# Opening tiles of a two-layer decoder trunk: the norm vector's two rows on another queue, and another order of the first tiles' work

## The chip, the cores and the metric

One core of one Trainium2 chip runs the whole program in one launch. The metric is the device time of that program in microseconds (us): the median of the runs shown, beside one profiled execution whose trace is read here. TensorE (PE in the profile) multiplies, VectorE (DVE) and ScalarE (ACT) do elementwise work, GpSimd (POOL) a little, and SyncE (SP) issues most loads. Each engine works its own list of instructions in order and waits for others by semaphores.

## The reference

A trunk of two layers on 512 tokens of width 1024, in float32. Each layer is a mixer, a cross-attention into 256 memory tokens and a SwiGLU feed-forward block, each with an RMS norm before and after it. The first layer's mixer is what the change is in:

```python
def fox_shortconv_mixer(h, w_in, b_f, conv_w, w_out):      # h = rmsnorm(x, g_mix_pre[0])
    proj = h @ w_in
    ...
    q, k, v, f_logit, b_gate, c_gate, u = jnp.split(proj, [i1, i2, i3, i4, i5, i6], axis=-1)
    ...
    log_f = jax.nn.log_sigmoid((f_logit + b_f).astype(jnp.float32))
    y_a = forgetting_attention(heads(q), heads(k), heads(v), log_f).reshape(bsz, seq, FOX_WIDTH)
    y_b = b_gate * causal_depthwise_conv(c_gate * u, conv_w)
    return jnp.concatenate([y_a, y_b], axis=-1) @ w_out
```

## The kernel before

Every float32 product is made of three products of rounded parts: high part times high part, high times low and low times high. In this stretch the names are `hTh` and `hTl` for the high and low part of the normed tokens (transposed), and `wh` and `wl` for those of the weights. ACT makes a high part by a cast, DVE makes the low part by subtracting it from the source.

The program begins with the value projection (`v`) of the first mixer, token tile by token tile (four tiles of 128 tokens, `x[0]` to `x[3]`). For a tile the squares are summed (half on ACT in `sumsq`, half on DVE), `rstd` raises the mean to the power -1/2 on POOL, `scaled` multiplies by that and by the norm's gain (DVE, tile `h`), and `put_T` transposes the eight 128x128 blocks on PE into two banks of four and splits each bank into `hTh` and `hTl`. The gain is needed on all 128 partitions: its two halves are loaded as two single rows into the tile `grow`, and two PE products with the 0/1 tile `pick` copy them to all partitions.

The weights of this projection come in four loads of 512 KB (`raw[0]`, `raw[2]`, `raw[4]`, `raw[6]`, tile `st`), each for two blocks of 128 rows. `whi_v(k0)` casts one of them on ACT (`wh`), `wlo_v(k0)` makes its low part on DVE (`wl`), and `mm_v(k0, t, which)` multiplies tile `t` with it: `h` is high by high, `x` is the low tokens by the high weights, `w` the high tokens by the low weights, two matmuls of 512 columns each, 24 for a tile. `warm_up(n)` is `n` transposes of a constant whose result nobody reads.

In this opening PE, ACT and DVE work in the order in which the Python code is written. From the gate logits on (`setup_chan` and what follows) only PE still does; the orders of ACT and DVE are there a scheduler's, which places instructions by its own estimates, so that an edit in the opening moves some of them too.

Behind the opening, the gate logits are one small product (tile `wf`), whose result ACT copies to `e` and DVE adds to `z`; the log-sigmoid and the running sum over the tokens follow on DVE (`log1p`, then a scan), the sum goes to DRAM (`cum`) by a POOL DMA, and for each pair of heads two POOL DMAs bring rows of it back to all partitions (`cb`). The first attention scores on PE fill banks that DVE empties with the help of `cb`. At the same time PE works through the `q`, `k` and convolution projections, whose results ACT and DVE split (`qk`).

Of the kernel before, what the change touches and what calls it, by code (L numbers as in the profile page):

```python
# [12 lines left out]
ALU = mybir.AluOpType  # L13
# [4 lines left out]
D = 1024  # L18
KT = D // P
# [14 lines left out]
WARM2 = 4  # L34
# [8 lines left out]
def trunk_kernel(ctx: ExitStack, tc: tile.TileContext, a: dict, out: bass.AP):  # L43
# [4 lines left out]
    nc = tc.nc  # L48
# [24 lines left out]
    def sbuf(name, n=512):  # L73
        return sp.tile([P, 516], F32, tag="s", name=name)[:, :n]

    def f(ap):
        return ap.bitcast(F32)
# [7 lines left out]
        out=mask, in_=mask, compare_op=ALU.is_ge, fill=1e30, base=0,  # L85
# [3 lines left out]
    grow = sbuf("grow")  # L89
# [9 lines left out]
    x = [xpool.tile([P, D], F32, name=f"x{t}", tag=f"x{t}") for t in range(NT)]  # L99

    def load_x(t):
        nc.sync.dma_start(out=x[t], in_=a["x"][0, t * P:(t + 1) * P, :])
# [16 lines left out]
    def load_raw(w, k0, nk, c0, c):  # L119
        st = wst.tile([P, nk, c], F32, tag="st", name="st")  # L120
        pace(nc.sync.dma_start(
            out=st, in_=w.rearrange("(k p) n -> p k n", p=P)[:, k0:k0 + nk, c0:c0 + c]
        ))
        return st
# [96 lines left out]
    def sumsq(src, acc):  # L221
        nc.scalar.activation(out=junk, in_=src, func=AF.Square, accum_out=acc)

    def rstd(st):

        nc.vector.tensor_scalar(
            out=st[:, 2:3], in0=st[:, 0:1], scalar1=1.0 / D, scalar2=EPS,
            op0=ALU.mult, op1=ALU.add,
        )
        nc.vector.scalar_tensor_tensor(  # L230
            out=st[:, 3:4], in0=st[:, 1:2], scalar=1.0 / D, in1=st[:, 2:3],
            op0=ALU.mult, op1=ALU.add,
        )
        pool[0] = nc.gpsimd.tensor_tensor(out=st[:, 4:5], in0=st[:, 3:4], in1=nhalf, op=ALU.pow).ins
        return st[:, 4:5]

    def stats(name):
        return tiny.tile([P, 8], F32, tag="st", name=name)

    def row_stats(xt, both=False):  # L240

        st = stats("pre")
        for hf in range(2):
            src = xt[:, hf * 512:(hf + 1) * 512]
            if both and hf:
                nc.vector.tensor_tensor_reduce(
                    out=sbuf("sq"), in0=src, in1=src, scale=1.0, scalar=0.0, op0=ALU.mult, op1=ALU.add,
                    accum_out=st[:, hf:hf + 1],
                )
            else:  # L250
                sumsq(src, st[:, hf:hf + 1])
        return rstd(st)

    def scaled(xt, g, r):

        hs = []
        for hf in range(2):
            h = sbuf("h")
            sl = slice(hf * 512, (hf + 1) * 512)
            nc.vector.scalar_tensor_tensor(  # L260
                out=h, in0=xt[:, sl], scalar=r, in1=g[hf], op0=ALU.mult, op1=ALU.mult
            )
            hs.append(h)
        return hs
# [10 lines left out]
    def new_hT():  # L275
        hi = [group("hTh") for _ in range(2)]
        lo = [group("hTl") for _ in range(2)]
        ft = Feat([hi[k // 4][:, k % 4, :] for k in range(KT)], [lo[k // 4][:, k % 4, :] for k in range(KT)])
        ft.ghi, ft.glo, ft.raw = hi, lo, None
        return ft  # L280
# [8 lines left out]
    def dst_T(hT, hf, t):  # L289
        if hT.hi:  # L290
            sl = slice(t * P, (t + 1) * P)
            return hT.ghi[hf][:, :, sl], hT.glo[hf][:, :, sl]
        q, c = hT.quads[hf][t // 2], t % 2 * P
        return q[:, :, c:c + P], q[:, :, 256 + c:256 + c + P]
# [5 lines left out]
        q = hT.quads[k // 4][half][:, k % 4, :]  # L300
        return q[:, 0:256], q[:, 256:512]

    def put_T(hT, t, hs, bank=bankB):
        for hf in range(2):
            ps = bank()
            for j in range(4):
                nc.tensor.transpose(
                    out=ps[:, j * P:(j + 1) * P], in_=hs[hf][:, j * P:(j + 1) * P], identity=ident
                )
            v = ps.rearrange("p (k c) -> p k c", k=4)  # L310
            sl = slice(t * P, (t + 1) * P)
            if hT.raw:
                nc.scalar.copy(out=hT.raw[hf][:, :, sl], in_=v)
            hi, lo = dst_T(hT, hf, t)
            last = (
                nc.scalar.copy(out=hi, in_=v).ins,  # L316
                nc.vector.tensor_tensor(out=lo, in0=v, in1=f(hi), op=ALU.subtract).ins,  # L317
            )
        return last
# [904 lines left out]
    def fox(proj):  # L1224
        w = a["ab_w_in"][0]
# [3 lines left out]
        hT = new_hT()  # L1229
# [6 lines left out]
        def warm_up(n):  # L1236
            for _ in range(n):
                nc.tensor.transpose(out=warm[:, 0:P], in_=ident, identity=ident)
# [4 lines left out]
        def mm_v(k0, t, which="hxw"):  # L1243

            ts = slice(t * P, (t + 1) * P)
            wh, wl = wv[k0]
            for c in which:
                for kk in range(2):
                    k = k0 + kk
                    passes[t] += 1  # L1250
                    nc.tensor.matmul(
                        out=banks[t], lhsT=(hT.lo if c == "x" else hT.hi)[k][:, ts],
                        rhs=(wl if c == "w" else wh)[:, kk, :], start=passes[t] == 1, stop=passes[t] == 3 * KT
                    )
            if passes[t] == 3 * KT:
                dst = vhl[t].rearrange("p (m s d) -> p m s d", s=4, d=64)
                src = banks[t].rearrange("p (m s d) -> p m s d", s=2, d=64)
                split_out(src, dst[:, :, 0::3, :], dst[:, :, 1:3, :])

        with tc.manual_schedule(engines={PE, mybir.EngineType.Activation, mybir.EngineType.DVE}):  # L1260
            load_x(0)
            for hf in range(2):
                nc.sync.dma_start(out=grow[32 * hf:32 * hf + 1], in_=a["g_mix_pre"][0:1, hf * 512:hf * 512 + 512])
            raw = {}
            for k0 in range(0, KT, 2):
                raw[k0] = load_raw(w, k0, 2, 2 * FOXW, 512)
                if k0 == 2:
                    load_x(1)
            load_x(2)
            load_x(3)  # L1270

            def whi_v(k0):
                hi = whi.tile([P, 2, 512], F32R, tag="wh", name="wh")
                lo = wlo.tile([P, 2, 512], F32R, tag="wl", name="wl")
                wv[k0] = hi, lo
                nc.scalar.copy(out=hi, in_=raw[k0])

            def wlo_v(k0):
                nc.vector.tensor_tensor(out=wv[k0][1], in0=raw[k0], in1=f(wv[k0][0]), op=ALU.subtract)

            nc.scalar.activation(out=junk[:, 0:1], in_=nhalf, func=AF.Square)
            g = bankB(), bankB()
            for hf in range(2):
                nc.tensor.matmul(out=g[hf], lhsT=pick[:, hf * P:hf * P + P], rhs=grow, start=True, stop=True)
            r = row_stats(x[0], True)
            nc.vector.tensor_copy(out=identb, in_=ident)
            hs = scaled(x[0], g, r)
            whi_v(0)
            wlo_v(0)
            put_T(hT, 0, hs)  # L1290
            warm_up(WARM2)
            mm_v(0, 0, "hwx")
            whi_v(2)
            r = row_stats(x[1], True)
            wlo_v(2)
            mm_v(2, 0, "hx")
            warm_up(WARM2)
            whi_v(4)
            mm_v(4, 0, "hx")
            hs = scaled(x[1], g, r)  # L1300
            wlo_v(4)
            mm_v(2, 0, "w")
            whi_v(6)
            put_T(hT, 1, hs)
            r = row_stats(x[2])
            mm_v(6, 0, "hx")
            wlo_v(6)
            hs = scaled(x[2], g, r)
            mm_v(0, 1, "hw")
            mm_v(2, 1, "hw")  # L1310
            mm_v(0, 1, "x")
            mm_v(2, 1, "x")
            mm_v(4, 0, "w")
            mm_v(4, 1)
            put_T(hT, 2, hs)
            r = row_stats(x[3])
            hs = scaled(x[3], g, r)
            mm_v(6, 0, "w")
            mm_v(6, 1)
            for k0 in range(0, KT - 2, 2):  # L1320
                mm_v(k0, 2)
            put_T(hT, 3, hs)
            mm_v(KT - 2, 2)
            for k0 in range(0, KT, 2):
                mm_v(k0, 3)
# [8 lines left out]
        for k in range(KT):  # L1334
# [5 lines left out]
            out=z, in0=ps[0:H], scalar=bf, in1=e, op0=ALU.add, op1=ALU.add  # L1340
# [5 lines left out]
            out=z, in0=z, scalar=0.0, in1=e, op0=ALU.min, op1=ALU.subtract  # L1346
# [3 lines left out]
            out=e, data0=t1, data1=z, initial=0.0, op0=ALU.mult, op1=ALU.add  # L1350
# [251 lines left out]
    hT = prev = None  # L1602
    for layer in range(2):
# [24 lines left out]
        hT = new_hT() if layer == 0 else None  # L1628
# [27 lines left out]
```

## Time and profile before

| | |
|---|---|
| median of 3 runs | 1387.04 us (1386.40 to 1387.37) |
| the profiled execution, its time | 1386.62 us |
| its span, first to last instruction | 1384.8 us |
| PE busy in the span | 1374.3 us (99%) |
| DVE, ACT, POOL busy | 80%, 52%, 8% |
| granted TensorE clock, mean | 0.998 of full speed |

The span is what the trace covers; 1.8 us of the execution's own time lie around it. Shares of busy time are means over the whole span. For a change in one place the timeline of that place is what counts, and whether the time won or lost there is still there at the end.

### The profile page before, as it was taken

To read this page: it belongs to the slowest core of one execution; us is meant where nothing else is said; L and a number is where in the kernel's file an instruction comes from. 1 tells how busy PE (TensorE), PEld (TensorE's weight loads), DVE (VectorE), ACT (ScalarE), POOL (GpSimd) and SP (SyncE) were. 2 spreads that over 40 slices of the span, in tenths; PEclk is the share of its full clock that TensorE was granted. 3 is DMA by queue.
4 is the path that set the end of the run, shared out by engine and by line. 5 is a ranking of instruction groups with operands and counts; after the bars stand their busy time and mean duration, and the time that the engine had idled before them with its cause. 6 is when DMAs were issued, how large, how long until landed. Compare 5 with 4: busy or idle time off the path is not lost.

```text
span 1384.8 us, 21780 instructions
## 1 busy us (share of the span) xinstructions
PE 1374.3 (99%) x8422; PEld 1225.1 (88%) x8422; DVE 1111.5 (80%) x1803; ACT 726.9 (52%) x1190; POOL 111.2 (8%) x160
## 2 busy tenths in 40 slices
PE   9999999999999999999999999999999999999998
PEld 7778788888899999998889888988889999999886
DVE  6775677546589999989898999663568999999987
ACT  5354456534464444456674797453446444445664
POOL 1000002012010101000011000101200011000001
PEclk9999999999999999999999999999999999999999
DMA  6845452668324557566665657356812555666654
GB/s 227 292 138 160 133 182 71 205 159 164 86 92 138 166 146 196 158 231 221 201 221 180 220 169 248 80 188 153 167 61 92 168 152 163 164 175 233 203 188 144
DMA packets 155108, 233.36 MB, mean 169 GB/s; under 512 B 8462, under 2 KB 90482, under 8 KB 153724
## 3 DMA queue, kind: packets, MB, share of 16 engines
q1 hardware_dynamic: 134420, 179.73, 39.6%
q0 software_dynamic: 17072, 46.16, 15.2%
q10 hardware_dynamic: 3512, 6.08, 1.5%
q8 instruction: 66, 1.08, 0.3%
q14 instruction: 38, 0.31, 0.1%
HBM read 219.34 MB, written 58.74 MB: 201 GB/s over the span
## 4 chain that ended last, share of the span: by engine, by line
PE 95%; issue 3%; DMA 1%; ACT 0%; DVE 0%; SPq 0%; POOL 0%; DVEq 0%; POOLq 0%; ACTq 0%
PE bA L338 13%; PE bA L340 13%; PE bA L339 13%; PE bB L338 6%; PE bB L339 6%; PE bB L340 6%; PE bB L814 3%; PE bB L812 3%; PE bB L813 3%; PE bA L814 2%; PE bA L812 2%; PE bA L813 2%; PE bA L571 2%; PE bA L573 2%; PE bB L571 2%
## 5 line engine op out<-in xcount | busy, mean ns | idle before, releaser
L548 DVE TENSOR_TENSOR wl<-st,wh 128x1024 fp32r<-128x1024 f32 x108 | 131.2, 1221 | 95.5 <-ACT wh L547 94.4
L547 ACT CAST wh<-st 128x1024 fp32r<-128x1024 f32 x108 | 113.2, 1050 | 119.1 <-PE bA L339 70.3
L338 PE MATMUL bA<-hTh,wh 128*128 128x512 f32 (+1 forms) x448 | 171.4, 383 | 0.2 <-ACT hTh L316 0.2
L339 PE MATMUL bA<-hTl,wh 128*128 128x512 f32 (+1 forms) x448 | 167.8, 375 | 0.3 <-DVE hTl L317 0.3
L340 PE MATMUL bA<-hTh,wl 128*128 128x512 f32 (+1 forms) x448 | 168.1, 375 | 0.0
L439 ACT CAST wg<-wr 128x1024 fp32r<-128x1024 f32 x80 | 83.6, 1045 | 48.9 <-DVE wr L468 38.5
L778 ACT CAST wh<-st 128x1024 fp32r<-128x1024 f32 x76 | 74.9, 986 | 63.7 <-PE bA L814 25.9
L340 PEld LDWEIGHTS bA<-hTh,wl 128*128 128x128 f32 x448 | 84.3, 188 | 15.4
L339 PEld LDWEIGHTS bA<-hTl,wh 128*128 128x128 f32 x448 | 84.6, 189 | 14.2 <-DVE hTl L317 0.5
L440 DVE TENSOR_TENSOR wg<-wr,wg 128x1024 fp32r<-128x1024 f32 x80 | 97.1, 1214 | 0.0
L338 PEld LDWEIGHTS bA<-hTh,wh 128*128 128x128 f32 x448 | 84.5, 189 | 14.0 <-ACT hTh L316 0.5
L783 DVE TENSOR_TENSOR wl<-st,wh 128x1024 fp32r<-128x1024 f32 x76 | 86.1, 1133 | 10.3 <-ACT wh L778 10.3
L439 ACT CAST wh<-tt 128x1024 fp32r<-128x1024 f32 x40 | 42.1, 1053 | 61.4 <-DVE tt L468 61.4
L338 PE MATMUL bA<-hTq,wh 128*128 128x256 f32 x208 | 59.2, 284 | 0.0
L340 PE MATMUL bA<-hTq,wl 128*128 128x256 f32 x208 | 58.9, 283 | 0.0
L339 PE MATMUL bA<-hTq,wh 128*128 128x256 f32 x208 | 58.8, 283 | 0.0
L812 PE MATMUL bB<-wh,ya 128*128 128x512 f32 x148 | 57.6, 389 | 0.0
L813 PE MATMUL bB<-wl,ya 128*128 128x512 f32 x148 | 57.6, 389 | 0.0
L814 PE MATMUL bB<-wh,ya 128*128 128x512 f32 x148 | 57.6, 389 | 0.0
L758 DVE TENSOR_TENSOR ya<-yb,ya 128x512 fp32r<-128x512 f32 x84 | 53.3, 638 | 0.0
L813 PE MATMUL bA<-wl,ya 128*128 128x512 f32 x132 | 51.3, 389 | 0.0
L814 PE MATMUL bA<-wh,ya 128*128 128x512 f32 x132 | 51.3, 389 | 0.0
(381 smaller groups left out, 4427.4 us busy)
## 6 DMA issues: line engine op xcount, KB each, us to landing
wr<-in_w_ffn_gu_dram SPq DMA_DIRECT2D x80, 512.0 KB
st<-t SPq DMA_DIRECT2D x40, 512.0 KB
t<-in_w_ffn_down_dram SPq DMA_DIRECT2D x32, 512.0 KB
st<-in_w_xkv_dram SPq DMA_DIRECT2D x32, 512.0 KB
st<-in_w_ffn_down_dram SPq DMA_DIRECT2D x30, 512.0 KB
st<-in_ab_w_in_dram SPq DMA_DIRECT2D x24, 512.0 KB
y<-yr POOLq DMA_DIRECT2D x18, 512.0 KB, 4.0
t<-in_w_ffn_down_dram POOLq DMA_DIRECT2D x16, 512.0 KB, 8.9
```

The source lines that it names most:

```text
L338: nc.tensor.matmul(out=ps, lhsT=wh, rhs=xh, start=first, stop=False)
L339: nc.tensor.matmul(out=ps, lhsT=wh, rhs=xl, start=False, stop=False)
L340: nc.tensor.matmul(out=ps, lhsT=wl, rhs=xh, start=False, stop=last)
L439: return (lambda: nc.scalar.copy(out=to[0], in_=src), lambda: nc.vector.tensor_tensor(out=to[1], in0=src, in1=f(to[0]), op=ALU.subtract))
L440: lambda: nc.vector.tensor_tensor(out=to[1], in0=src, in1=f(to[0]), op=ALU.subtract))
L547: nc.scalar.copy(out=hi, in_=src)
L548: nc.vector.tensor_tensor(out=lo, in0=src, in1=f(hi), op=ALU.subtract)
L778: nc.scalar.copy(out=self.wt[s][0], in_=self.st[s])
L783: nc.vector.tensor_tensor(out=lo, in0=self.st[s], in1=f(hi), op=ALU.subtract)
L812: nc.tensor.matmul(out=banks[t], lhsT=yh, rhs=wh[:, jj, :], start=first and jj == 0, stop=False)
L813: nc.tensor.matmul(out=banks[t], lhsT=yh, rhs=wl[:, jj, :], start=False, stop=False)
L814: nc.tensor.matmul(out=banks[t], lhsT=yl, rhs=wh[:, jj, :], start=False, stop=last and jj == n - 1)
```

## The change

The two rows of the norm's gain are loaded from ACT's queue instead of SP's, so that SP issues the first weight load right after `x[0]`. Of the two groups of four `warm_up` transposes in the opening one is left. The casts of the first two weight loads both stand ahead of the first tile's splits on ACT. The squares of the second tile, its `rstd` and the low part of the first weights stand between the two halves of the first tile's `put_T` (the new argument `between`). On PE the products of high parts come first, for the first tile and then for the second, and the products with low weights later. From the third tile on the order on PE is the same as before.

```diff
-    def put_T(hT, t, hs, bank=bankB):
+    def put_T(hT, t, hs, bank=bankB, between=None):
         for hf in range(2):
+            if hf and between:
+                between()
             ps = bank()
...
             for hf in range(2):
-                nc.sync.dma_start(out=grow[32 * hf:32 * hf + 1], in_=a["g_mix_pre"][0:1, hf * 512:hf * 512 + 512])
+                nc.scalar.dma_start(out=grow[32 * hf:32 * hf + 1], in_=a["g_mix_pre"][0:1, hf * 512:hf * 512 + 512])
...
             whi_v(0)
-            wlo_v(0)
-            put_T(hT, 0, hs)
+            whi_v(2)
+            st1, r1 = stats("pre"), []
+            src = x[1][:, 512:D]
+            nc.vector.tensor_tensor_reduce(
+                out=sbuf("sq"), in0=src, in1=src, scale=1.0, scalar=0.0, op0=ALU.mult, op1=ALU.add,
+                accum_out=st1[:, 1:2],
+            )
+
+            def norm_1():
+                sumsq(x[1][:, 0:512], st1[:, 0:1])
+                r1.append(rstd(st1))
+                wlo_v(0)
+
+            put_T(hT, 0, hs, between=norm_1)
+            for c in "hx":
+                for k0 in (0, 2):
+                    mm_v(k0, 0, c)
+            whi_v(4)
             warm_up(WARM2)
-            mm_v(0, 0, "hwx")
-            whi_v(2)
-            r = row_stats(x[1], True)
+            mm_v(4, 0, "h")
+            hs = scaled(x[1], g, r1[0])
+            mm_v(0, 0, "w")
+            whi_v(6)
+            mm_v(6, 0, "h")
             wlo_v(2)
-            mm_v(2, 0, "hx")
-            warm_up(WARM2)
-            whi_v(4)
-            mm_v(4, 0, "hx")
-            hs = scaled(x[1], g, r)
-            wlo_v(4)
-            mm_v(2, 0, "w")
-            whi_v(6)
             put_T(hT, 1, hs)
             r = row_stats(x[2])
-            mm_v(6, 0, "hx")
+            mm_v(4, 0, "x")
+            mm_v(6, 0, "x")
+            wlo_v(4)
+            for k0 in range(0, KT, 2):
+                mm_v(k0, 1, "h")
+            mm_v(0, 1, "w")
+            for t in range(2):
+                mm_v(2, t, "w")
             wlo_v(6)
             hs = scaled(x[2], g, r)
...
```

In the built programs this moves instructions at three places. In the rows below lines of the changed kernel are 2 higher than those of before up to the opening, and 15 to 17 higher behind it.

First, ACT in the opening, before: from the sum of squares of the first tile (`x_112`) to the splits of the first tile and the casts of the weights.

```order
L222 ACTIVATE junk,pre<-x_112 128x512
L1276 CAST wh<-st 128x1024
L316 CAST hTh<-bB 128x4x128 x2
L1276 CAST wh<-st 128x1024
L222 ACTIVATE junk,pre<-x_113 128x512
L1276 CAST wh<-st 128x1024 x2
```

And ACT in the same place, now:

```order
L222 ACTIVATE junk,pre<-x_112 128x512
L1278 CAST wh<-st 128x1024 x2
L318 CAST hTh<-bB 128x4x128
L222 ACTIVATE junk,pre<-x_113 128x512
L318 CAST hTh<-bB 128x4x128
L1278 CAST wh<-st 128x1024 x2
```

The second weight cast moved ahead of both splits of the first tile, and the sum of squares of the second tile (`x_113`) between them.

DVE in the same stretch, before, from the scaled first tile on (`ISA sq` is the sum of squares):

```order
L260 SCALAR_TENSOR_TENSOR h<-x_112,pre,bB 128x512 x2
L1279 TENSOR_TENSOR wl<-st,wh 128x1024
L317 TENSOR_TENSOR hTl<-bB,hTh 128x4x128 x2
L246 ISA sq,pre<-x_113 128x512
L246 ISA pre 128x1
```

DVE in the same stretch, now:

```order
L260 SCALAR_TENSOR_TENSOR h<-x_112,pre,bB 128x512 x2
L1294 ISA sq,pre<-x_113 128x512
L1294 ISA pre 128x1
L319 TENSOR_TENSOR hTl<-bB,hTh 128x4x128
L226 TENSOR_SCALAR pre<-pre 128x1
L230 SCALAR_TENSOR_TENSOR pre<-pre 128x1
L1281 TENSOR_TENSOR wl<-st,wh 128x1024
L319 TENSOR_TENSOR hTl<-bB,hTh 128x4x128
L260 SCALAR_TENSOR_TENSOR h<-x_113,pre,bB 128x512 x2
```

The squares of the second tile stand ahead of the first `hTl`, and the first weights' low part behind it, between the halves.

Second, ACT where the gate logits come out of PE, before (`COPY e` reads them; the casts are weights of later projections):

```order
L547 CAST v<-bA 128x4x2x64
L209 ACTIVATE lt_413<-chan 128x8
L210 ACTIVATE lt_413<-lt_413 128x8
L1338 COPY e<-bA 8x512
L547 CAST wh<-st 128x1024
```

ACT there, now:

```order
L549 CAST v<-bA 128x4x2x64
L549 CAST wh<-st 128x1024
L209 ACTIVATE lt_409<-chan 128x8
L210 ACTIVATE lt_409<-lt_409 128x8
L549 CAST wh<-st 128x1024
L1355 COPY e<-bA 8x512
```

A weight cast that stood behind the copy of the logits stands ahead of it; DVE's subtraction for that cast stands now ahead of its `z`, too.

Third, DVE around the first steps of the log-sigmoid and at its end, before, in two pieces (the second ends with the scan, L1349):

```order
L181 RECIPROCAL t_461<-t_461 8x512
L548 TENSOR_TENSOR wl<-st,wh 128x1024
L182 TENSOR_TENSOR t_462<-e,t_461 8x512
L551 SCALAR_TENSOR_TENSOR qk<-bA,qk 128x512
L183 TENSOR_TENSOR t_461<-t_462 8x512
L184 TENSOR_SCALAR e<-t_461 8x512
```

```order
L186 SCALAR_TENSOR_TENSOR e<-e,t_461 8x512 x3
L190 SCALAR_TENSOR_TENSOR e<-e,t_462 8x512
L1348 MEMSET t_461 8x512
L1345 SCALAR_TENSOR_TENSOR z<-z,e 8x512
L548 TENSOR_TENSOR wl<-st,wh 128x1024
L1349 SCALAR_TENSOR_TENSOR e<-t_461,z 8x512
L548 TENSOR_TENSOR qk<-bA,qk 128x512
```

DVE at the same two pieces, now (the scan is L1366):

```order
L181 RECIPROCAL t_457<-t_457 8x512
L553 SCALAR_TENSOR_TENSOR qk<-bA,qk 128x512
L182 TENSOR_TENSOR t_458<-e,t_457 8x512
L550 TENSOR_TENSOR wl<-st,wh 128x1024
L183 TENSOR_TENSOR t_457<-t_458 8x512
L553 SCALAR_TENSOR_TENSOR qk<-bA,qk 128x512
L184 TENSOR_SCALAR e<-t_457 8x512
```

```order
L550 TENSOR_TENSOR wl<-st,wh 128x1024
L186 SCALAR_TENSOR_TENSOR e<-e,t_457 8x512 x2
L550 TENSOR_TENSOR qk<-bA,qk 128x512
L190 SCALAR_TENSOR_TENSOR e<-e,t_458 8x512
L1365 MEMSET t_457 8x512
L1362 SCALAR_TENSOR_TENSOR z<-z,e 8x512
L1366 SCALAR_TENSOR_TENSOR e<-t_457,z 8x512
```

A `qk` that waits for PE's `q` product stands now right behind the reciprocal, and three of the `qk` splits instead of two stand ahead of the scan; `wl` subtractions stand three times between reciprocal and scan, in both.

## Rows read from the trace of the kernel before

**Rows 1.** The page: the chain that ended last, and one group of instructions.

```profile
PE 95%; issue 3%; DMA 1%; ACT 0%; DVE 0%; SPq 0%; POOL 0%; DVEq 0%; POOLq 0%; ACTq 0%
...
L548 DVE TENSOR_TENSOR wl<-st,wh 128x1024 fp32r<-128x1024 f32 x108 | 131.2, 1221 | 95.5 <-ACT wh L547 94.4
```

**Rows 2.** What PE waited for behind 35 us: us, times, longest.

```profile
PE bB L1404 <- DVE fx L1411: 0.4, 1, 0.4
```

**Rows 3.** Timeline of PE: start, us, instructions, idle before them.

```profile
1.47 3.03 PE L1238 MATMUL bA<-ident 128*128 128x128 f32 x13 [1.47 <-POOL ident masks.py:199]
...
6.91 1.31 PE L307 MATMUL bB<-ident,h 128*128 128x128 f32 x8 [0.46 <-DVE h L260]
...
8.46 0.73 PE L1251 MATMUL bA<-wh,hTh 128*128 128x512 f32 x2
...
9.83 0.73 PE L1251 MATMUL bA<-wh,hTl 128*128 128x512 f32 x2
...
14.18 1.03 PE L307 MATMUL bB<-ident,h 128*128 128x128 f32 x8
...
35.01 0.27 PE L205 MATMUL bB<-ident,rows 128*128 128x128 f32 x1
```

**Rows 4.** Timeline of SP's queue: issue, and its length.

```profile
0.74 0.39 SPq L102 DMA_DIRECT2D x<-in_x_dram  x1
1.43 0.58 SPq L1263 DMA_DIRECT2D grow<-in_g_mix_pre_dram  x2
2.05 0.91 SPq L121 DMA_DIRECT2D st<-in_ab_w_in_dram  x2
```

**Rows 5.** Timeline of ACT in the opening.

```profile
4.26 0.63 ACT L222 ACTIVATE junk<-x 128x512 bf16<-128x512 f32 x1 [1.40 <-DMA x<-in_x_dram]
...
6.88 1.05 ACT L1276 CAST wh<-st 128x1024 fp32r<-128x1024 f32 x1 [1.89 <-DMA st<-in_ab_w_in_dram]
7.83 1.06 ACT L316 CAST hTh<-bB 128x512 fp32r<-128x512 f32 x2
8.93 1.05 ACT L1276 CAST wh<-st 128x1024 fp32r<-128x1024 f32 x1
10.28 0.63 ACT L222 ACTIVATE junk<-x 128x512 bf16<-128x512 f32 x1 [0.30 <-DMA x<-in_x_dram]
...
11.58 1.04 ACT L1276 CAST wh<-st 128x1024 fp32r<-128x1024 f32 x1 [0.58 <-DMA st<-in_ab_w_in_dram]
```

**Rows 6.** Timeline of DVE in the opening.

```profile
9.10 1.28 DVE L317 TENSOR_TENSOR hTl<-bB,hTh 128x512 fp32r<-128x512 f32 x2
10.29 0.68 DVE L246 CUSTOM_DVE_ANT_0 sq<-x 128x512 f32<-128x512 f32 x1
```

**Rows 7.** Timelines of ACT and DVE from the gate logits to the scan.

```profile
39.00 0.58 ACT L1338 COPY e<-bA 8x512 f32<-8x512 f32 x1 [2.37 <-PE bA L1336]
...
41.09 0.63 ACT L1343 ACTIVATE e<-e 8x512 f32<-8x512 f32 x1
...
42.77 3.34 DVE L181 RECIPROCAL t<-t 8x512 f32<-8x512 f32 x1
...
47.82 0.69 DVE L551 SCALAR_TENSOR_TENSOR qk<-bA,qk 128x512 fp32r<-128x512 f32 x1
...
58.42 1.21 DVE L1349 TENSOR_TENSOR_SCAN e<-t,z 8x512 f32<-8x512 f32 x1
```

**Rows 8.** The chain that ended last, 59 to 71 us: start, us, what.

```profile
59.93 2.49 DMA cum<-e
...
63.55 6.64 DMA cb<-cum
...
70.68 0.44 PE bB L1404
```

**Rows 9.** The tile cb: its eight DMAs from issue to landing.

```profile
DMA to landing us min/median/max: 3.3/3.7/6.6
```

**Rows 10.** One us at the end: busy PE, PEld, DVE, ACT, POOL, granted clock, DMA.

```profile
1380.00:1381.00 1.00, 0.00 (x0) 0.00 (x0) 0.96 (x3) 0.00 (x0) 0.00 (x0) 0.70 0.00 0
```

More of the change, by code (lines that the diff above doesn't have):

```diff
@@ L1288, in fox @@
             whi_v(0)
-            wlo_v(0)
-            put_T(hT, 0, hs)
-            warm_up(WARM2)
-            mm_v(0, 0, "hwx")
-            whi_v(2)
-            r = row_stats(x[1], True)
-            wlo_v(2)
-            mm_v(2, 0, "hx")
-            warm_up(WARM2)
-            whi_v(4)
-            mm_v(4, 0, "hx")
-            hs = scaled(x[1], g, r)
-            wlo_v(4)
-            mm_v(2, 0, "w")
-            whi_v(6)
+            whi_v(2)
[14 more added lines that the diff above has]
+            whi_v(4)
+            warm_up(WARM2)
+            mm_v(4, 0, "h")
[3 more added lines that the diff above has]
+            mm_v(6, 0, "h")
+            wlo_v(2)
             put_T(hT, 1, hs)
             r = row_stats(x[2])
-            mm_v(6, 0, "hx")
+            mm_v(4, 0, "x")
[6 more added lines that the diff above has]
+                mm_v(2, t, "w")
             wlo_v(6)
             hs = scaled(x[2], g, r)
[L1309 to L1314, printed above, removed]
+            for k0 in range(0, KT, 2):
+                mm_v(k0, 1, "x")
+            for t in range(2):
+                mm_v(4, t, "w")
             put_T(hT, 2, hs)
@@ L1317, in fox @@
             hs = scaled(x[3], g, r)
-            mm_v(6, 0, "w")
-            mm_v(6, 1)
+            for t in range(2):
+                mm_v(6, t, "w")
             for k0 in range(0, KT - 2, 2):
```

## The prediction

> **What bounds the kernel now.** I read the page's chain first. 95% of what ended last is TensorE, and DMA, ACT and DVE hold about 1% together [rows 1]. Then what PE waits for behind 35 us: at scores (`bB` L1404) that wait for DVE to empty a bank, once, 0.4 us [rows 2]. A kernel whose PE is dense from 35 us to the end has no place to make up for a delay or to swallow a gain. Whatever moves the end of the value projection, the product at 35.01 [rows 3], moves the end of the program by as much, except at the one wait, which can absorb up to 0.4 us of a delay of PE or grow. So two numbers decide: how much later or earlier PE reaches the product at 35.01, and how long the wait at 70.68 becomes.
>
> How much is there to win in the opening? Tile 0's transposes begin at 6.91 and the projection ends at 35.01, 28.1 us later. Later transposes take 1.03 for eight, 0.129 each [rows 3]. From 14.18 to 35.01 PE does 24 transposes and 80 products (16 of the 96 are done by then) in 20.83 us, so a product takes (20.83 - 24 x 0.129) / 80 = 0.222. Without any wait the whole would be 96 x 0.222 + 32 x 0.129 = 25.4, so 2.7 us is the most that any order could win behind 6.91. That is just 0.2% of the time (2.77 us), which is about what a measurement of this kernel can tell from no change. And it is out of reach, since the first product needs a cast of the first weights, which land after 6 us now.
>
> **The loads.** SP issues `x` at 0.74, `grow` from 1.43 on for 0.58, and `st` from 2.05 on [rows 4]. With `grow` gone, `st` follows at 0.74 + 0.39, say 1.17, so 0.88 earlier. `grow` on ACT costs nothing: ACT has its first work at 4.26, after 1.40 us without any, and PE needs the gain only behind its 13 opening transposes, which end at 4.50 [rows 3, 5]. If that cover were gone, the cost would be the issue's 0.58. What does the earlier issue bring? `x` is seen at 4.26 and the first weights at 6.88, 2.6 later; in the steady stream two successive loads, `x` of the second tile and `st`, are seen at 10.28 and 11.58, both after idle time that a DMA ended, 1.3 apart [rows 5]. If the first pair closed up to that distance, the first weights would be there at 4.26 + 1.3 = 5.5, and all loads 1.35 earlier; if it is the data path and not the issue that makes the 2.6, nothing moves. Bounds 0 and 1.35, the issue alone 0.88. I take 0.4, nearer to nothing, because the later loads come at the stream's own pace, which an earlier issue does not quicken.
>
> [...]
>
> **ACT in the opening.** Before, ACT casts the first weights at 6.88, splits both halves of tile 0 from 7.83 on, and casts the second weights at 8.93 [rows 5]. Now that second cast stands ahead of the splits. Its load can't be seen much before 8.93: the next one is seen at 10.28, and the stream's step is 1.3. So the first half of `hTh` begins at 8.93 + 0.95 = 9.88, two us later, and the first product, 0.63 behind the start of `hTh` before (8.46 against 7.83), at 10.5 [rows 3, 5], less the loads' shift.
>
> **DVE in the opening.** Before, `hTl` begins at 9.10, its product at 9.83, and the squares of `x_113` at 10.29, as soon as it landed [rows 3, 6]. Now those squares stand ahead of `hTl`, so that `hTl` waits for the load of tile 1: 10.28 + 0.68 and some 0.07 to its start is 11.03, and the first `x` products follow 0.73 later, at 11.76. The four products ahead of them start at 10.5 and take 0.9, so PE waits there again. From 11.76 on, dense, there are 92 products, 24 transposes and four warm-ups: the 20.83 of before, 12 x 0.222 = 2.66 and 4 x 0.129 = 0.5, together 24.0, which ends at 35.8 instead of 35.01: +0.8. Tile 1's transposes now follow close behind DVE work that stands in a row (`rstd`'s steps, `wl`, `hTl`, `h`); for that I allow 0.3, with bounds 0 and one `wl`, 1.2 [rows 1]. Opening: +1.1 with loads as before, **+0.7** with my shift of 0.4, +0.2 with 0.88, -0.2 with 1.35.
>
> **The gate chain.** This is the part that the diff does not show. ACT's copy of the gate logits started at 39.00, as soon as PE had them, after 2.37 idle [rows 7]. Now a weight cast stands ahead of it that begins no earlier than the copy did: +1.05 (a cast's time, [rows 5]). DVE's `z` stands behind that cast's `wl`, 1.22 [rows 1], which runs while ACT copies; I carry +1.05 to the end of the reciprocal, 42.77 + 3.34 = 46.11 before, 47.1 now. Directly behind it DVE's list now has a `qk` that needs PE's `q` product, and before that `qk` ran at 47.82 [rows 7]: another +0.7 in which DVE waits, and the rest of the log-sigmoid is queued behind it. One more `qk` stands ahead of the scan: +0.69. For the next `qk`'s own wait I allow 0.2. Sum +2.6: the scan, which ended at 58.42 + 1.21 = 59.63, ends 2.6 later in relation to PE. Bounds: 1.05 + 0.69 = 1.7 if the `qk` waits are filled, 3.4 if the second waits as long as the first.
>
> Behind the scan come the DMA of `cum` (2.49), the first DMA of `cb` (6.64), DVE's work, and PE at 70.68 [rows 8], which waits 0.4 there already [rows 2]: the chain has no slack, and its +2.6 reaches PE but for what the DMAs give back. The 6.64 is the slowest of eight such DMAs; their median is 3.7 and the fastest 3.3 [rows 9]. What made the first slow no row shows; it is the one issued while the weights of the projections stream in, and its place against them moves. Between 0 and 2.9 of it (6.6 - 3.7) may come back; I take 1.2, nearer to the row of this very DMA. Net +1.4, so PE's one wait would be 1.8 instead of 0.4.
>
> **Sum.** +0.7 + 2.6 - 1.2 = +2.1 on the profiled execution's 1386.62: 1388.7. The median is 0.42 above that execution, by which it would be 1389.1. I take **1388.9**.
>
> **Rivals.**
> - *Loads close up and `cb` is quick.* For it: 0.88 of issue time is really removed, and 3.7 is `cb`'s usual time. Against it: the stream's pace. Opening +0.2, chain 2.6 - 2.9, of which nothing is left but a wait of 0.1: about +0.3 or less, 1387.1; with the shift of 1.35 and no wait at all at `bB` it is -0.2 - 0.4 = -0.6, 1386.4.
> - *The whole chain arrives.* Loads not earlier, `cb` at 6.64 as before: 1.1 + 2.6 = +3.7, 1390.5. It decides as slower from 2.77 on, that is, when `cb` gives back under 0.9.
> - *The clock.* PE's transposes end at 6.91 + 1.31 = 8.22 and it now has nothing till about 10, where before warm-ups and products came. [...] The 13 transposes at the start took 3.03, or 0.233 each, against 0.129 later [rows 3]: the products would lose about 13 x 0.104 = 1.4 until the clock is back, so +3.5, 1390.3. It decides from an idle stretch in which the granted clock falls at all. [...]
> - *Faster by more than 0.2%*: all of the opening's 2.7 won and no wait at `bB`. The first weights' landing excludes nearly all of it.
>
> **Chances.** The sum, from +1.0 to +2.7: 0.50. Loads and `cb` quick: 0.20. Both end within 0.2% of 1387.04 (up to 1389.81). The whole chain: 0.17. The clock: 0.11. Faster: 0.02. So slower 0.28, same 0.70. The range goes from the quick rival's lower end, 1386.4, to a little over the slow ones, 1391.0; the likeliest case alone has 1387.8 to 1389.8.
>
> **What the changed kernel's profile would show.** SP's first `st` issue near 1.17. ACT's first weight cast between 5.5 and 6.9, by which I read the shift (6.5 by mine). First product near 10 instead of 8.46, `x` products near 11.4, `ident,rows` near 35.7. The copy of `e` with a cast of 1.05 ahead of it, a `qk` behind the reciprocal with a wait of about 0.7 on PE, the scan's end near 62.9. The first `cb` DMA near 5.4. One wait of PE at the scores of about 1.8. A granted clock of 1.00 from 8 to 14 us. I would be wrong if tile 1's load comes so much earlier that the squares don't hold up `hTl`, if ACT's second cast waits longer for its load than 8.93, or if `cb`'s time follows another rule than these.

## The result, and the profile after

| | before | after |
|---|---|---|
| median of 12 runs | 1387.41 us (1385.87 to 1388.03) | 1390.81 us (1390.05 to 1391.53) |
| ratio, 95% interval | | 1.0025 (1.0018 to 1.0033) |
| the profiled execution | 1386.62 us, span 1384.8 | 1391.19 us, span 1389.4 |

The change costs 3.4 us, a little more than the 2.8 (0.2%) from which the prediction counts it as slower, and near the upper end of the range. In the profiled executions it is 4.6. PE's timeline of after shows where these come in:

```profile
1.47 3.04 PE L1240 MATMUL bA<-ident 128*128 128x128 f32 x13 [1.47 <-POOL ident masks.py:199]
5.70 3.75 PE L1286 MATMUL bB<-grow,pick 128*128 128x512 f32 x4 [1.20 <-DMA grow<-in_g_mix_pre_dram]
9.24 1.71 PE L309 MATMUL bB<-ident,h 128*128 128x128 f32 x8
10.86 1.20 PE L1253 MATMUL bA<-wh,hTh 128*128 128x512 f32 x4
11.89 1.08 PE L1253 MATMUL bA<-wh,hTl 128*128 128x512 f32 x4
...
35.95 0.27 PE L205 MATMUL bB<-ident,rows 128*128 128x128 f32 x1
...
71.90 0.44 PE L1421 MATMUL bB<-qk 64*128 64x384 f32 x1 [1.02 <-DVE fx L1428]
73.40 0.76 PE L1421 MATMUL bB<-qk 64*128 64x384 f32 x5 [1.06 <-DVE fx L1428]
...
78.86 0.29 PE L1424 MATMUL bB<-mask,identb 128*128 128x128 bf16 x2
...
232.53 1.18 PE L309 MATMUL bA<-ident,h 128*128 128x128 f32 x7 [0.67 <-DVE h L260]
```

The rows of before that these are held against, beside those in [rows 3] and [rows 8]:

```profile
4.30 2.15 PE L1284 MATMUL bB<-grow,pick 128*128 128x512 f32 x4
...
74.97 0.28 PE L1407 MATMUL bB<-mask,identb 128*128 128x128 bf16 x2
...
227.94 1.29 PE L307 MATMUL bA<-ident,h 128*128 128x128 f32 x8
```

Row by row against before: `ident,rows` 35.95 against 35.01 [rows 3], +0.94; the scores behind the wait 73.40 against 70.68 [rows 8], +2.72; the mask behind the next scores 78.86 against 74.97, +3.89; the transposes 232.53 against 227.94, +4.59. From there the difference stays. So there are four places: the opening +0.9, the waits at the scores +1.8, the stretch right behind them +1.2, and a wait at 231.9, +0.7.

The opening, on the queues of SP and ACT and on ACT:

```profile
1.19 0.93 SPq L121 DMA_DIRECT2D st<-in_ab_w_in_dram  x2
...
1.44 0.55 ACTq L1265 DMA_DIRECT2D grow<-in_g_mix_pre_dram  x2
...
6.30 1.04 ACT L1278 CAST wh<-st 128x1024 fp32r<-128x1024 f32 x1 [1.45 <-DMA st<-in_ab_w_in_dram]
7.86 1.04 ACT L1278 CAST wh<-st 128x1024 fp32r<-128x1024 f32 x1 [0.52 <-DMA st<-in_ab_w_in_dram]
10.22 0.59 ACT L318 CAST hTh<-bB 128x512 fp32r<-128x512 f32 x1 [1.31 <-PE bB L309]
```

The weights are issued and land earlier, as forecast. But the rows, issued at the same time as before (1.44 for 1.43, [rows 4]), now reach PE at 5.70 instead of behind the transposes at 4.30. And the four pick products take 3.75 us instead of 2.15 (before: 4.30 to 6.45). Only then come the transposes, and ACT's split waits for PE.

The gate chain and what follows it, on ACT and DVE:

```profile
39.94 1.05 ACT L549 CAST wh<-st 128x1024 fp32r<-128x1024 f32 x1 [1.91 <-PE bA L1353]
41.02 0.58 ACT L1355 COPY e<-bA 8x512 f32<-8x512 f32 x1
...
44.79 3.34 DVE L181 RECIPROCAL t<-t 8x512 f32<-8x512 f32 x1
48.76 0.69 DVE L553 SCALAR_TENSOR_TENSOR qk<-bA,qk 128x512 fp32r<-128x512 f32 x1 [0.63 <-ACT qk L552]
...
62.09 1.21 DVE L1366 TENSOR_TENSOR_SCAN e<-t,z 8x512 f32<-8x512 f32 x1
63.23 0.65 DVE L550 TENSOR_TENSOR qk<-bA,qk 128x512 fp32r<-128x512 f32 x1
63.81 1.20 DVE L550 TENSOR_TENSOR wl<-st,wh 128x1024 fp32r<-128x1024 f32 x1
71.55 0.29 DVE L1428 CUSTOM_DVE_ANT_0 p<-bB,cb 128x128 f32<-128x128 f32 x1 [6.53 <-DMA cb<-cum]
71.76 0.08 DVE L1428 DVE_READ_ACCUMULATOR2_ANT fx<- 128x1 f32 x1
71.76 1.22 DVE L550 TENSOR_TENSOR wl<-st,wh 128x1024 fp32r<-128x1024 f32 x1
...
72.97 0.27 DVE L1428 CUSTOM_DVE_ANT_0 p<-bB,cb 128x128 f32<-128x128 f32 x1
```

The scan ends at 63.30 instead of 59.63 [rows 7]. The first `p` waits for `cb`, and the second stands behind a `wl`: these are PE's two waits, 1.02 and 1.06, where before there was one of 0.4 [rows 2]. The `wl` at 63.81 matters too: SP's next weight load waits for it to free its tile, and is issued at 65.08 (29.1 behind `ident,rows`; before at 62.90, 27.9 behind). The chain that ended last has the transfers (of the two `cb` of the first pair of heads this is the first; the row in [rows 8] is the second), and the table of windows (columns as in [rows 10]) what PE's clock did behind the waits:

```profile
63.60 1.95 DMA cum<-e
...
66.10 5.31 DMA cb<-cum
```

```profile
74.00:75.00 1.00, 1.00 (x7) 0.83 (x6) 0.93 (x7) 0.92 (x4) 0.00 (x0) 0.89 0.73 147
75.00:76.00 1.00, 1.00 (x4) 0.72 (x4) 1.00 (x7) 0.48 (x1) 0.00 (x0) 0.50 1.08 386
76.00:77.00 1.00, 1.00 (x4) 0.81 (x3) 0.96 (x6) 1.00 (x5) 0.00 (x0) 0.50 1.06 411
77.00:78.00 1.00, 1.00 (x5) 0.35 (x5) 0.45 (x2) 0.30 (x1) 0.00 (x0) 0.50 0.33 121
78.00:79.00 1.00, 1.00 (x9) 0.59 (x9) 0.00 (x0) 0.00 (x0) 0.00 (x0) 0.91 0.00 0
```

The granted clock is 0.50 for three us, although PE is busy without a gap there; the gaps lie just ahead. That is the +1.2 of this profile. Of the twelve executions nine have a mean granted clock of 0.997 over the whole run (median 1391.05), three have 0.999 (1390.05, 1390.33 and 1390.42). So the clock seems to fall in most executions and not in all, and those three are still 2.9 above the kernel before; where it fell in executions without a trace is not shown.

### The profile page after: what moved, and what is told of

It is laid out like the page before. It is cut to its first block, busy times and chain, and to the rows that moved or that the text cites. A ratio compares the mean times of both kernels' runs of the same rounds, so it can differ in the third digit from the quotient of the medians.

```text
span 1389.4 us, 21776 instructions
## 1 busy us (share of the span) xinstructions
PE 1376.5 (99%) x8418; PEld 1226.5 (88%) x8418; DVE 1111.5 (80%) x1803; ACT 727.0 (52%) x1190; POOL 111.1 (8%) x160
## 4 chain that ended last, share of the span: by engine, by line
PE 95%; issue 3%; DMA 1%; DVE 1%; ACT 0%; POOL 0%; DVEq 0%; POOLq 0%; ACTq 0%
PE bA L340 13%; PE bA L342 13%; PE bA L341 13%; PE bB L341 6%; PE bB L340 6%; PE bB L342 6%; PE bB L815 3%; PE bB L814 3%; PE bB L816 3%; PE bA L815 2%; PE bA L814 2%; PE bA L816 2%; PE bA L573 2%; PE bA L575 2%; PE bA L574 2%
## 5 line engine op out<-in xcount | busy, mean ns | idle before, releaser
L816 PE MATMUL bA<-wh,ya 128*128 128x512 f32 x132 | 51.4, 389 | 0.0
L814 PE MATMUL bA<-wh,ya 128*128 128x512 f32 x132 | 51.4, 389 | 0.0
```

Of the source, the lines that this page charges most:

```text
L814: nc.tensor.matmul(out=banks[t], lhsT=yh, rhs=wh[:, jj, :], start=first and jj == 0, stop=False)
L816: nc.tensor.matmul(out=banks[t], lhsT=yl, rhs=wh[:, jj, :], start=False, stop=last and jj == n - 1)
```

## The experiments

Medians stand beside those of the kernel before on the same chip. One execution of these kernels differs from the next by 1 us or more, so differences under about 1 us are not told apart by the intervals. The ratio is not the quotient of the two medians; where the two differ much (e4, e5), both are given.

**Rows back on SP's queue (e1), logits' copy first (e2), both (e3).** The edit of e1 is one word, that of e2 an edge of order for one weight cast (in the list of casts behind the logits, the fourth):

```diff
-                nc.scalar.dma_start(out=grow[...], in_=a["g_mix_pre"][...])
+                nc.sync.dma_start(out=grow[...], in_=a["g_mix_pre"][...])
```

```diff
     def split_w(st, nk, c):
...
-        split_out(st, hi, lo)
+        with ExitStack() as order:
+            if fence:
+                for ins in fence.pop(0):
+                    order.enter_context(tc.issue_after(ins))
+            split_out(st, hi, lo)
...
+        fence.extend([(), (), (), (proj.gate, zi)])      # zi: DVE's z
```

e1: 

> The changed kernel with the two rows of the norm's gain back on SP's queue, ahead of the weights; all else as changed. ACT's and DVE's lists are those of the changed kernel. Theory 1 (in the opening two effects cancel: the first weights land about 1.1 us earlier, but the rows land 1.5 us later, PE stands idle for 1.2 us and does the four pick products at half speed, 3.75 us instead of 2.15): pick products at 4.3 again, first weight cast near 6.9, second-tile squares wait for their load, ident,rows between 35.7 and 36.1, total within 0.5 us of the changed kernel. Rival (the late rows are all that the opening loses): ident,rows at 35.0 to 35.2 and about 0.9 us less than the changed kernel.

e2: 

> The changed kernel with one edge of order: the fourth weight cast behind the gate logits stays behind ACT's copy of the logits, and its low part behind DVE's z. The opening is as changed (ident,rows near 35.95). Theory (the gate chain, which arrives late at PE's one wait, carries most of the loss): the scan ends near 60.6 instead of 63.3, PE waits at the scores 0.4 us or less instead of 2.1, the granted clock stays at 1.00 behind it, and the total is 2.3 to 3.2 us less than the changed kernel, so 0.5 to 1.0 above the kernel before. Rival (the delay of the chain is swallowed by the transfers, and the time is lost in the opening): less than 0.8 us less.

e3: 

> Both edits, the rows on SP and the logits' copy first. What is left of the change is the order of the first tiles' work. Theory 1 (the order by itself costs 0.8 to 1.1 us because the second cast and the second tile's squares stand ahead of the first tile's splits): 0.7 to 1.2 above the kernel before. Rival (the order is free, only the late rows and the gate chain cost): within 0.3 us of the kernel before.

With the one edge of e2 the scheduler puts the rest of the chain back into the order of before by itself: no `qk` right behind the reciprocal, two ahead of the scan, no `wl` between the two `p`.

| | median, us | before there | ratio to before, 95% |
|---|---|---|---|
| e1 | 1391.48 | 1387.45 | 1.0033 (1.0020 to 1.0046) |
| e2 | 1387.20 | 1387.45 | 1.0000 (0.9991 to 1.0009) |
| e3 | 1388.14 | 1387.45 | 1.0004 (0.9995 to 1.0013) |

e2 takes the whole loss away, 3.6 us, a little more than the expected 2.3 to 3.2. Its `ident,rows` and its scan:

```profile
36.18 0.27 PE L211 MATMUL bB<-ident,rows 128*128 128x128 f32 x1
...
59.95 1.21 DVE L1373 TENSOR_TENSOR_SCAN e<-t,z 8x512 f32<-8x512 f32 x1
```

The scan ends at 61.16, 25.0 behind `ident,rows` (before 24.6, after 27.35), and PE waits for nothing at the scores. The rival that put the loss into the opening has fallen. With the rows on SP the total is 0.7 (e1 against after) and 0.9 (e3 against e2) higher than without, which the intervals don't tell from nothing; e3, 0.7 above the kernel before, fits theory 1 and does not exclude the rival. In e1 PE waits at the scores as in after, 1.12 and 1.06, and the granted clock is 0.50 for six us behind that instead of three. In e3, whose scan is as early as in e2, PE still waits 1.0 there. The opening of e1 ended at 35.34, that of e3, the same program up to there, at 37.25: neither window for `ident,rows` was met, because the opening is not the same from one execution to the next.

The profile of e3, the slowest of its eleven executions (1390.49), has the opening that the prediction described. PE's timeline, and two windows (columns as in [rows 10]) with its clock:

```profile
10.44 1.21 PE L1259 MATMUL bA<-wh,hTh 128*128 128x512 f32 x4 [2.24 <-ACT hTh L324]
11.51 2.07 PE L1259 MATMUL bA<-wh,hTl 128*128 128x512 f32 x4
```

```profile
12.00:13.00 1.00, 1.00 (x4) 0.71 (x4) 1.00 (x2) 0.57 (x1) 1.00 (x1) 0.50 1.00 397
13.00:14.00 1.00, 1.00 (x5) 0.80 (x4) 1.00 (x2) 0.69 (x1) 0.26 (x1) 0.50 0.69 275
```

With the rows on SP the transposes are early (6.88), ACT's second cast (8.86) holds up the first split (9.81), and the squares of the second tile wait 2.67 for their load (10.15). PE stands for 2.24, and then the granted clock falls to 0.50: four products take 2.07 where e1's take 1.20. In after the late rows hide these steps.

**The rows on ACT in the kernel before (e4), and as ACT's first transfers (e7, e10).** e4 is the edit of e1 the other way round, in the kernel before. e7 moves the issue ahead and reads each row from its own partition, so that no clearing is needed; e10 is the same in e2:

```diff
-    nc.vector.memset(grow, 0.0)
-    nc.vector.memset(pick, 0.0)
+    for hf in range(2):
+        nc.scalar.dma_start(out=grow[32 * hf:32 * hf + 1], in_=a["g_mix_pre"][...])
...
-                nc.tensor.matmul(out=g[hf], lhsT=pick[:, hf * P:hf * P + P], rhs=grow, ...)
+                nc.tensor.matmul(out=g[hf], lhsT=pick[32 * hf:32 * hf + 1, hf * P:hf * P + P],
+                                 rhs=grow[32 * hf:32 * hf + 1], ...)
```

e4: 

> The kernel before with one edit, the two rows on ACT's queue and the weights right behind the first tile on SP's. ACT's and DVE's lists keep their order, at the gate logits too. Theory (the rows queue behind the weights' packets in the DMA engines): rows seen at 5.6 to 5.8 instead of before 4.3, the pick products at half speed for 3.7 us, first product near 10.9 instead of 8.46, weights 0.6 to 1.1 earlier, ident,rows at 36.0 to 36.6, total 1.0 to 1.6 above the kernel before. Rival (the queue is harmless, the transfer runs on the same DMA engines anyway): within 0.3 of the kernel before, or lower by the 0.6 that the weights come sooner.

e7: 

> The kernel before with the two rows as ACT's very first transfers, ahead of the first weights. For that the clearing of the rows' tile, for which the transfer would have to wait, is dropped, and each pick product reads only the one partition that holds its row. All lists but for that are as before. Theory (it matters which of the transfers comes first, not which queue issues it): rows as early as before (pick products at 4.3), the first weights about 0.6 and the later ones about 1.1 us earlier, ident,rows at 33.9 to 34.6 instead of 35.0, total 0.4 to 1.1 below the kernel before. Rival (a later transfer on ACT's queue is behind the first tile's and weights' packets in any case): rows late as in the changed kernel, total 0.8 above.

e10: 

> The changed kernel with the logits' copy first and with the rows as ACT's first transfers, not waiting for the clearing of their tile (each pick product reads one partition). Theory (rows and weights are both early then): pick products at 4.4, tile 0's transposes at 7.4, first weight cast near 6.3, second near 7.9, first product near 9.6 instead of 11.05, ident,rows between 34.6 and 35.3, total 0.5 to 1.2 below the run with the logits' copy first. Rival (with the first product two us behind the transposes PE idles and runs at half speed for some us, so that nothing is won): total within 0.4 of that run.

e4: 1388.26 against 1387.45, ratio 1.0010 (1.0001 to 1.0018). That is 0.8 above by the medians, between theory and rival, and 1.4 by the ratio, as the theory had it; the interval (0.1 to 2.5) does not tell the two apart. Its pick products begin at 5.73, as in after, and `ident,rows` comes at 37.03, later than the theory's 36.6. In e7, with the rows on the same queue but issued ahead of the weights, they begin at 4.44. So the rows are late because they stand behind the weights, and not because of who issues them. (In e7 they are also issued 0.7 earlier, at 0.74, but their products begin 1.3 earlier. The rows on SP behind the weights were not tried.) The trace of after agrees: the four packets of the rows (queue q10) move between 3.5 and 5.5, two us in which the packets of SP's queue (q1) take 100% of the time of the 16 DMA engines, and the rows land 3.87 after their second issue at 1.70.

But e7 won nothing: 1388.03 against 1387.24, ratio 1.0004 (0.9995 to 1.0013), with `ident,rows` at 35.57 instead of 33.9 to 34.6. That is the rival's 0.8 above, but not for its reason, since the rows are early. And e10 lost, 1389.38 against 1387.42, ratio 1.0015 (1.0006 to 1.0024), which is 2.2 above e2 and outside both its theory and its rival. PE's timeline of e10:

```profile
4.43 2.29 PE L1290 MATMUL bB<-grow,pick 1*128 1x512 f32 x4
7.44 1.97 PE L315 MATMUL bB<-ident,h 128*128 128x128 f32 x8 [0.72 <-DVE h L266]
9.40 2.08 PE L1259 MATMUL bA<-wh,hTh 128*128 128x512 f32 x4
11.28 1.91 PE L1259 MATMUL bA<-wh,hTl 128*128 128x512 f32 x4
```

The first product comes at 9.40, as the theory had it, 1.5 us ahead of after's. Then four products take 2.08, where after needs 1.20 for the same four. `ident,rows` comes at 36.61. What the early data won, PE's lower rate took back in this execution, with a granted clock that reads 1.00 throughout the opening. In five of the eleven executions the mean granted clock is 0.996 (1389.54 to 1390.28), in five 0.999 (1387.55 to 1389.38), and in the profiled one 0.998; if the clock fell in the first five, no trace shows where.

**One `wl` behind the second `p` (e5).** The ninth cast behind the logits gets an edge to DVE's second `p`; all ahead of it stays as changed.

> The changed kernel with one edge of order elsewhere: the low part of the ninth weight cast behind the logits stays behind the second of DVE's two p that empty the first scores' banks. Everything ahead of the scores, the late scan too, is as changed. Theory (PE's second wait of 1.06 us is that subtraction alone, and the two waits in a row are what let the clock fall to half for three us): one wait of about 1.0 us is left, the granted clock stays near 1.00 behind it, and the total is 2.0 to 2.4 us below the changed kernel. Rival A (the clock falls with the first wait already): only the second wait is saved, 1.0 to 1.2 us. Rival B (DVE is late anyway): under 0.5 us.

1389.49 against 1387.24, ratio 1.0012 (1.0003 to 1.0021): 1.3 below after by the medians, 1.8 by the ratios, between theory and rival A. In its profile PE waits 1.4 at the scores, 1.2 in one piece, and the granted clock reads 1.00 in each us from 73 to 77. With 0.2 left of the second wait the clock does not fall, in this execution; of the eleven, one has a mean granted clock of 0.997, where after has nine of twelve.

**The scan done three times in the kernel before (e6).**

```diff
-        nc.vector.tensor_tensor_scan(
+        for _ in range(3):
+            nc.vector.tensor_tensor_scan(
```

> The kernel before with DVE's scan over the tokens done three times with the same operands, so that the running sum is ready 2.4 us later and nothing ahead of it moves. Opening and queues as before. Theory (the gate chain sets the time of PE's wait at the scores, so what it loses reaches the end): the wait grows from 0.4 to between 1.5 and 2.9 us, depending on what the transfers give back, and the total by 1.3 to 2.5, or by up to 3.7 if the clock falls to half behind the wait. Rival (the transfers behind the scan swallow it): less than 0.6 us more than the kernel before.

The theory fell: 1387.47 against 1387.24, ratio 0.9999 (0.9991 to 1.0008).

```profile
61.01 2.45 DVE L1350 TENSOR_TENSOR_SCAN e<-t,z 8x512 f32<-8x512 f32 x2
```

The running sum is as late as in after (63.46, 27.6 behind `ident,rows` at 35.88), and PE waits only 0.6 at the scores. A late scan by itself is swallowed by the transfers: the second `cb` takes 4.5 instead of 6.6 and lands 35.4 behind `ident,rows` (before 35.2). Note `ident,rows`: 35.88 in a program whose opening is that of before, 35.01.

**The copy of 512 KB next to cb (e9, and e11 in the kernel before).** SP issues a copy `t` beside most weight loads. It was left out at the one load (the thirteenth) next to which `cb` is issued, and follows later:

```diff
-        if loads[0] > 0 and loads[0] % (COPIES + 1) and copies:
+        if loads[0] > 0 and loads[0] % (COPIES + 1) and loads[0] != LATER and copies:
```

e9: 

> The changed kernel without the one copy of 512 KB (tile t, DRAM to DRAM) that SP issues half a microsecond ahead of the cb transfers; it and those behind it come one weight load later. Orders of ACT, DVE and PE as changed, so the scan is as late and the subtraction still stands between the two p. Theory (in every run so far the second cb landed 7.0 us, give or take 0.5, after SP's weight load at that place, however late the scan was, so it is the data issued around it that sets the landing): the second cb lands 0.7 to 1.5 us earlier than 72.05, the first wait of PE at the scores falls from 1.02 to under 0.4, the clock doesn't fall behind it, total 1.5 to 2.7 below the changed kernel. Rival (cb takes its own time from its issue, 5.3 us): landing, waits and total as changed, within 0.5 us.

e11: 

> The kernel before without the copy of 512 KB (tile t) next to the cb transfers, moved one weight load later. One look, for the landing alone. Theory: the second cb lands 34.0 to 34.6 us behind the product ident,rows instead of 35.2, and PE does not wait at the scores. Rival: 35.2 and a wait of 0.4 as before.

e9: 1388.56 against 1387.42, ratio 1.0008 (0.9999 to 1.0017), 2.25 below after, as the theory had it. Three views of e9, the waits of PE, the tile `cb`, and PE's timeline:

```profile
PE bB L1422 <- DVE fx L1429: 0.8, 1, 0.8
```

```profile
DMA to landing us min/median/max: 3.4/3.7/4.0
```

```profile
5.64 1.96 PE L1287 MATMUL bB<-grow,pick 128*128 128x512 f32 x4 [1.13 <-DMA grow<-in_g_mix_pre_dram]
7.66 1.43 PE L310 MATMUL bB<-ident,h 128*128 128x128 f32 x8
```

The slowest of the eight `cb` transfers takes 4.0 instead of 5.4 in after. In e11 the second `cb` takes 5.1 instead of 6.6 before [rows 9]. So the copy beside it makes 1.4 to 1.5 of its time in either kernel, and not all that the 6.6 has over the others. Counted from SP's weight load at that place, the second `cb` lands 6.7 to 8.0 later in the eleven profiles with the copy (e3 and e8, 8.0 and 7.8, lie outside the 7.0 give or take 0.5 of the expectation), and 5.3 to 5.6 later in the three without it. PE waits once, 0.8 (for the second `p`, with the `wl` ahead of it, instead of under 0.4 for the first), and the clock stays at 1.00 behind it. e11, a single run: 1386.84, the second `cb` lands 33.5 behind `ident,rows` (before 35.2, expected 34.0 to 34.6), and PE does not wait at the scores. The last rows are of the opening: the rows land as late as in after and PE idles 1.13, but here the pick products take 1.96 instead of 3.75 and the transposes 1.43 instead of 1.71.

**More opening transposes (e8), and three edits at once (e12).** e8 is e2 with `WARM = 20` instead of 13; e12 is e8 with the edit of e9.

e8: 

> The changed kernel with the logits' copy first and with 20 instead of 13 opening transposes, so that PE is busy until the rows land. Theory (the pick products take 3.75 us because PE stood idle for 1.2 us before them and runs at half speed): they take about 2.2 us, tile 0's transposes begin near 8 instead of 9.3, the first product comes near 10 instead of 11.05, ident,rows near 35.2, total 0.7 to 1.2 below the run with the logits' copy first alone. Rival (the products are slow because the transfers or the rows' tile make them so): 3.75 us still, same total.

e12: 

> The changed kernel with three edits that stood alone so far: the logits' copy first, 20 opening transposes, and the copy of 512 KB next to the cb transfers one weight load later. Theory (each takes away a loss of its own): no wait of PE at the scores, no fall of the clock there, the first product near 10, total 0.3 to 1.2 below the kernel before. Rival (what is left of these losses was already within what one run differs from the next): within 0.3 of the kernel before.

e8: the pick products begin at 5.84 without idle time and take 2.74, not 3.75, `ident,rows` comes at 35.12. The total is 1387.24 against 1387.24, ratio 0.9996 (0.9987 to 1.0005): not told apart from e2, against an expected 0.7 to 1.2 less. e12: 1385.67 against 1387.30, ratio 0.9987 (0.9978 to 0.9996), the one kernel whose interval lies below the kernel before. PE's timeline of e12:

```profile
5.83 2.04 PE L1293 MATMUL bB<-grow,pick 128*128 128x512 f32 x4
7.94 1.42 PE L316 MATMUL bB<-ident,h 128*128 128x128 f32 x8
9.67 1.20 PE L1260 MATMUL bA<-wh,hTh 128*128 128x512 f32 x4 [0.31 <-ACT hTh L325]
```

PE waits nowhere at the scores, where e8 had one wait of 0.8. The gain is 1.6 us, more than the expected 0.3 to 1.2.

## Why the prediction was right, and where it was wrong

The range held the time, 0.2 below its upper end, but the likeliest case (no change that can be told) did not come; the side with 28 in 100 did. That the range held is in part luck: the opening's 0.7 is not in the medians, and in its place stand a `wl` that was not counted and a fall of the clock that was expected elsewhere.

- *Loads.* Right in the issue (1.19 for 1.17) and the first cast (6.30 for about 6.5). Wrong that the rows on ACT's queue cost nothing: the cover, PE's opening transposes to 4.50, was there, but behind the weights the rows reach PE 1.3 to 1.4 us later (e4 against e7, after against before). The reading that ACT has its first work at 4.26 was wrong as well, since a table load stands at 1.37; the issues move it to 2.01, which holds up nothing.
- *Opening, +0.7.* Measured +0.94 in the profiles, but not by the steps given: DVE's squares of the second tile never waited for their load (they begin at 10.15, behind `h`), it was the rows, and the four pick products, which took 3.75 instead of 2.15. With the rows on SP (e3) the steps come as given: split 9.81 for 9.88, first product 10.44 for 10.5, `x` products 11.51 for 11.76. And neither profile is typical. The opening of before ended at 35.01 and, in e6, at 35.88, that of after at 35.95 and, in e9, at 34.58. By the medians, e2 has only the opening changed, and its ratio is 1.0000 with 0.9 in a thousand on either side: the term is nothing, or up to 1.2 us either way.
- *Gate chain, +2.6 at the scan.* Right: 63.30 - 35.95 = 27.35 against 24.62, +2.73, and step by step: the cast ahead of the copy (39.94), the reciprocal's end 48.13 (47.1 with the opening's 0.94 on top is 48.04), the wait of the `qk` 0.63 for 0.7. (The upper bound of 3.4 is 3.1 by its own terms.)
- *What the transfers give back, 1.2.* The 6.64 was taken for the first `cb`; it is the second of the pair. That one, which set PE's wait before, landed at 70.19 [rows 8], 35.2 behind `ident,rows`, and lands at 72.05, 36.1 behind it, so 1.8 of the 2.7 came back. But after's first wait is set by the first `cb`, which landed at 68.45, 33.4 behind, and lands at 71.41, 35.5 behind: there only 0.7 came back. e6, with as late a scan, shows nothing left in the total. The runs fit a landing that follows SP's weight load and the copy beside it (e6, e9, e11) more than the scan.
- *PE's wait, 1.8.* Measured 2.1, but in two: the second is the `wl` between the two `p`. That `wl` was in DVE's new list, and the prediction did not count it; e5 puts it at 1.3 to 1.8 in the total, together with the clock.
- *The clock.* The rival had the fall and the price (1.4; measured 1.2 for the three us at 0.50), but put it into the gap at 8 to 10 us. In after it came behind the two waits at the scores. In e3's profile it came where the rival had it, behind a gap of 2.24 from 8.2 to 10.4, and `ident,rows` is 1.9 later than in e1, of which the first product has 0.55. A fall where PE stands, before shows at its end: PE's last product ends at 1378.00, and the granted clock is 1.00 up to 1380, 0.70 in the next us [rows 10] and 0.50 from 1381 on. How long PE has to stand is not shown: behind waits of 1.02 and 1.06 it fell in after, behind one of 1.2 it did not in e5.
- *The 0.7 at 231.9* had no step, and needs none: a wait of 0.4 to 1.2 us for `h` at this place stands in twelve of the fourteen profiles, in that of e11 (opening and chain of before) too. The profile of before was one of the two without it.

So the loss is that of the gate chain's order: one weight cast, ahead of the logits' copy, and what the scheduler put behind it, with the weight load that waits for DVE there. e2 shows it, by undoing just that: its load is back at 27.9 behind `ident,rows`. How the 3.4 split between first wait, `wl` and clock is read from single profiles, and e5 and e9 (1.3 to 1.8, and 2.25) fit it only roughly. Why a scan as late cost nothing in e6 is shown in part: there the copy was issued 29.1 behind `ident,rows` instead of 29.55 in after, and no `wl` stood between the `p`. That the copy's place alone makes the rest of the difference was not tried.

## What to carry to other kernels

An edit in code whose order is fixed by hand can move work tens of us further on, where a scheduler decides, so compare the lists of all engines and cost every place where a short dependent chain gets a long independent instruction ahead of it. Count also what stands between two instructions for which the same engine waits twice: two waits of 1 us in a row cost more than their sum in two profiles here (after, e1): the granted clock was 0.50 for three and six us behind them. And where transfers follow a chain, ask first what else is issued beside them; moving one copy won 2.25 us in e9 against after and 1.6 in e12 against e8, and no edit of the opening won anything that can be told.

## What was not expected of the hardware

- The granted clock does not tell all. It reads 1.00 in every us of the opening, in after as in before (of the fourteen profiles only e3's shows a fall there), while the first transposes take 0.23 each (13 in 3.04) against 0.13 later (eight in 1.03). But its record begins only at 4.83 us in before and at 9.92 in after, and time without a record reads 1.00. Up to there only the durations show the lower rate.
- When the opening gets to the higher rate differs between executions of the same instructions: with idle time of 1.20 and 1.13 ahead of them, the same four pick products took 3.75 in after and 1.96 in e9. The first product comes 1.7 earlier by it, and `ident,rows` at 34.58 instead of 35.95. No run here shows what decides it.
